# A decoder block's first norm: scale and shift in eight pieces, and a turn of x by diagonal matmuls

## The chip, the cores and the metric

The kernel runs on one core of a Trainium2 chip. A time is the device time of one execution in microseconds; the number compared is the median over several executions. Profiled executions are single ones, with a trace.

## What is computed

A decoder block over 256 tokens of width 1024: a modulated norm, a token mixer (attention and a gated convolution), a second modulated norm and a mixture of 32 experts. The change touches only how the first norm and its modulation are made, ahead of the projection `w_in`:

```
mod = jax.nn.silu(c) @ w_ada[l] + b_ada[l]
sh1, sc1, ga1, sh2, sc2, ga2 = jnp.split(mod, N_MOD, axis=-1)
h = modulate(rms_norm(x, g_norm1[l]), sh1, sc1)    # norm(x) * (1 + sc1) + sh1
z = h @ w_in[l]
```

`c` is one row of 1024, `w_ada` is 1024 x 6144, so `sc1` and `sh1` are 1024 values each, and each needs 1024 x 1024 weights (4 MB).

## The kernel before, in words

**Order of transfers.** All large weights come in through SP's queue, in one list (`stream`), into a ring of slots of 1 MB (`slots`; `pump` at lines 125 to 138 sends as long as a slot is free, `release` frees one and pumps). For the front, `FIRST` (line 40) writes the order by hand: four pieces of 256 columns for the scale (`sc1.i`), four for the shift (`sh1.i`), and eight row blocks of `w_in` for q, k and v (`qkv.k`, 768 KB), mixed as `sc0 sh0 qk0 sc1 qk1 sh1 ...`. Small rows (`c`, `b_ada`, `g_norm1` and others) go through the same queue (`load_rows`, line 222). A DMA of this queue may also have to wait for an earlier DMA's completion, eight places before it in program order: the waits named `DMAHW0` to `DMAHW7`.

**Start.** `x` (two tiles of 128 tokens) is squared on VectorE and ScalarE (lines 353, 355), the inverse root is made (lines 356 to 358), x is scaled by it (`xh`, lines 360, 361) and transposed by 16 TensorE transposes into four PSUM banks (line 365), which VectorE and ScalarE copy to `hf` (lines 372, 374). Between the two halves of the transposes stand the first pieces of scale and shift: `first_ada` (lines 509 to 525) makes eight matmuls of 32 x 256 (four column groups of the array side by side, line 516), copies the bank to `part` and turns it into columns by two matmuls with `sel` (line 501, "cols" below), after which VectorE makes `a1` or `sh1` (lines 504 to 507). `warm(n)` issues n idle matmuls.

**Units.** The front's matmul work is a list of units: 24 for q, k and v (three per k, each six matmuls of 512 columns, line 428, in three products of high and low parts), then 56 for the other projections and more. Each unit's weights are split into a high part by ScalarE (line 396, `sthi`) and a low part by VectorE (line 397, `stlo`), four units ahead at most (`run_units`, lines 401 to 417). Tasks are generators: `after(i, g)` starts one behind unit i, and each unit advances every task by one step, so a task's instructions stand between the units on every engine. `first_scale(i)` and `first_shift(i)` for i = 1 to 3 are such tasks. Scale pieces 2 and 3 are summed on VectorE (`ada_sum`, lines 331, 333), all others on TensorE. `modulate1(k)` (lines 527 to 530) makes the high part of the modulated x on ScalarE, then the value and its low part on VectorE; unit 3k needs them. `small_work` (lines 561 to 576, behind unit 7) transposes small rows in banks 6 and 7.

**Behind the front** come attention, convolution, the second norm, routing (from line 939) and eight rounds of four experts (lines 1049 to 1207), each reading 24 MB of weights through the same ring. `L1027` gathers tokens with matmuls that have a block of x as the stationary operand and 128 columns of a one-hot matrix as the moving one.

```
    for i in range(1, 4):
        after(6 * i - 6, lambda i=i: first_scale(i))
        after(6 * i - 3, lambda i=i: first_shift(i))
```

## Time and profile before

| | |
|---|---|
| median of 3 runs | 663.52 us (663.48 to 663.66) |
| the profiled execution | 665.23 us, of which its span is 663.5 us |
| TensorE busy | 533.8 us (80%) |
| VectorE, ScalarE, GpSimd busy | 195.5, 146.7 and 40.9 us |
| read from HBM | 257.12 MB, 389 GB/s over the span |
| SP's queue | 256.98 MB, 93.4% of 16 engines' span |

The page cuts the span into 40 slices of 16.6 us; a digit is a busy share in tenths. The span begins with the first instruction and ends with the last one; the execution's own time has 1.7 us more around it.

### The profile page before, as it was taken

To read this page: it belongs to the slowest core of one execution; us is meant where nothing else is said; L and a number is where in the kernel's file an instruction comes from. 1 tells how busy PE (TensorE), PEld (TensorE's weight loads), DVE (VectorE), ACT (ScalarE), POOL (GpSimd) and SP (SyncE) were. 2 spreads that over 40 slices of the span, in tenths; PEclk is the share of its full clock that TensorE was granted. 3 is DMA by queue.
4 is the path that set the end of the run, shared out by engine and by line. 5 is a ranking of instruction groups with operands and counts; after the bars stand their busy time and mean duration, and the time that the engine had idled before them with its cause. 6 is when DMAs were issued, how large, how long until landed. Compare 5 with 4: busy or idle time off the path is not lost. (4 is left out here: it accounts for less than half of the span.)

```text
span 663.5 us, 11736 instructions
## 1 busy us (share of the span) xinstructions
PE 533.8 (80%) x5054; PEld 322.1 (49%) x5055; DVE 195.5 (29%) x405; ACT 146.7 (22%) x290; POOL 40.9 (6%) x59
## 2 busy tenths in 40 slices
PE   7999999999999899988575756676766875677765
PEld 6678897988998637363043104301510540161033
DVE  4687449657896412020020001001100100010002
ACT  4536456744555220010010001000000100010001
POOL 0012511500040000000000000000000000000000
PEclk9999999999999898999888799968987596897669
DMA  8999994699959699999999997999999999999996
GB/s 315 426 425 398 426 421 154 244 356 378 399 199 407 282 410 426 425 427 424 428 427 423 423 426 328 423 428 427 425 426 426 428 426 425 428 425 425 427 427 255
DMA packets 37765, 259.01 MB, mean 390 GB/s; under 512 B 4545, under 2 KB 5673, under 8 KB 7242
## 3 DMA queue, kind: packets, MB, share of 16 engines
q1 hardware_dynamic: 36136, 256.98, 93.4%
q10 hardware_dynamic: 1362, 1.05, 0.5%
q8 instruction: 42, 0.69, 0.4%
q0 software_dynamic: 208, 0.15, 0.1%
q14 instruction: 17, 0.14, 0.1%
HBM read 257.12 MB, written 1.05 MB: 389 GB/s over the span
## 5 line engine op out<-in xcount | busy, mean ns | idle before, releaser
L1060 PE MATMUL ps<-slot,xg 128*32 128x512 f32 x1024 | 163.4, 745 | 76.4 <-DMA slot<-in_up_dram 71.4
L1060 PEld LDWEIGHTS ps<-slot,xg 128*32 128x32 f32 x1024 | 26.1, 120 | 197.8 <-DMA slot<-in_up_dram 160.3
L428 PE MATMUL ps<-hbuf,sthi 128*128 128x256 f32 x512 | 94.8, 287 | 0.0
L428 PEld LDWEIGHTS ps<-hbuf,sthi 128*128 128x128 f32 x512 | 79.0, 190 | 11.4 <-ACT sthi L396 6.7
L397 DVE TENSOR_TENSOR stlo<-slot,sthi 128x512 fp32r<-128x512 f32 x100 | 72.0, 723 | 37.9 <-ACT sthi L396 36.7
L396 ACT ACTIVATE sthi<-slot 128x512 fp32r<-128x512 f32 x108 | 68.0, 630 | 62.7 <-PE ps L428 50.2
L1068 DVE TENSOR_TENSOR sl<-sl,ps 128x512 f32<-128x512 f32 x8 | 5.5, 688 | 254.7 <-PE ps L1060 246.4
L1080 PE MATMUL ps<-slot,sl 128*32 128x128 f32 x2048 | 67.9, 287 | 14.6 <-DMA slot<-in_down_dram 9.7
L428 PE MATMUL ps<-hbuf,stlo 128*128 128x256 f32 x256 | 72.2, 282 | 0.7 <-POOL stlo L397 0.7
L1080 PEld LDWEIGHTS ps<-slot,sl 128*32 128x32 f32 x2048 | 57.1, 115 | 29.1 <-DMA slot<-in_down_dram 13.3
L1047 ACT ACTIVATE GW<-ps 128x256 f32<-128x256 f32 x8 | 3.1, 384 | 239.1 <-PE ps L1046 239.1
L1088 PE MATMUL ps<-ysb,GW 128*128 128x512 f32 (+1 forms) x76 | 37.1, 615 | 17.6 <-DVE ysb L1086 17.6
L428 PEld LDWEIGHTS ps<-hbuf,stlo 128*128 128x128 f32 x256 | 48.5, 190 | 0.9 <-POOL stlo L397 0.9
L428 PE MATMUL ps<-sthi,hbuf 128*128 128x512 f32 x128 | 43.2, 404 | 1.1 <-ACT hbuf L528 0.9
L1086 DVE TENSOR_TENSOR ysb<-ps,ga 128x512 f32<-128x512 f32 (+1 forms) x19 | 11.5, 606 | 90.7 <-PE ps L1080 83.7
L1027 PEld LDWEIGHTS ps<-GW,x 128*128 128x128 f32 x256 | 33.4, 212 | 6.4 <-issue 5.6
L1027 PE MATMUL ps<-GW,x 128*128 128x128 f32 x256 | 36.0, 302 | 0.2 <-DVE GW L1018 0.2
L1088 PEld LDWEIGHTS ps<-ysb,GW 128*128 128x128 f32 x76 | 13.3, 203 | 30.9 <-DVE ysb L1086 22.1
L428 PEld LDWEIGHTS ps<-sthi,hbuf 128*128 128x128 f32 x128 | 23.7, 188 | 8.9 <-issue 1.6
L1033 ACT ACTIVATE xg<-ps,sm,sm 128x128 f32<-128x128 f32 x32 | 12.4, 457 | 59.8 <-PE ps L1027 59.8
L428 PE MATMUL ps<-stlo,hbuf 128*128 128x512 f32 x64 | 25.1, 392 | 0.0
L1035 DVE TENSOR_SCALAR xg<-ps,sm,sm 128x128 f32<-128x128 f32 x32 | 11.2, 404 | 35.0 <-PE ps L1027 35.0
(264 smaller groups left out, 429.2 us busy)
## 6 DMA issues: line engine op xcount, KB each, us to landing
slot<-in_up_dram SPq DMA_DIRECT2D x128, 1024.0 KB, 19.6
slot<-in_down_dram SPq DMA_DIRECT2D x64, 1024.0 KB, 19.6
slot<-in_front_dram SPq DMA_DIRECT2D x42, 1024.0 KB, 11.4
slot<-in_front_dram SPq DMA_DIRECT2D x8, 768.0 KB, 14.4
gates<-in_front_dram SPq DMA_DIRECT2D x4, 1024.0 KB, 7.0
x<-in_x_dram SPq DMA_DIRECT2D x2, 512.0 KB, 3.7
out_dram<-x ACTq DMA_DIRECT2D x1, 512.0 KB
out_dram<-x ACTq DMA_DIRECT2D x4, 128.0 KB, 1.8
```

What stands on the lines that cost most here:

```text
L396: S.activation(hi, src, AF.Copy)
L397: (G if i in on_pool else V).tensor_sub(lo, src, hi.bitcast(F32))
L428: PE.matmul(o, l, r, start=start and n == 0, stop=stop and n == 2, skip_group_check=True)
L1027: PE.matmul(o[:, 128 * (k % 4):128 * (k % 4) + 128], x[:, t, 128 * k:128 * k + 128], Gt[:, t, :], start=t == 0, stop=t == 1)
L1033: S.activation(xg[:, k, :], src, AF.Identity, bias=sh2[:, k:k + 1], scale=a2[:, k:k + 1])
L1035: V.tensor_scalar(xg[:, k, :], src, a2[:, k:k + 1], sh2[:, k:k + 1], op0=OP.mult, op1=OP.add)
L1047: S.activation(WT.rearrange("p t n -> p (t n)"), YC[:, :256], AF.Copy)
L1060: PE.matmul(o[js, :], xg[:, k, js], w[:, j, :], start=k == 0, stop=k == DK - 1)
L1068: V.tensor_mul(sl, sl, HB)
L1080: PE.matmul(bank[js, cs], hidT[:, k, js], w[:, 4 * j + k, :], start=k == 0, stop=k == 3, skip_group_check=True)
L1086: V.tensor_mul(ysb[:, cs], (bank or (YC, YD)[n])[:, cs], ga2[:, ns])
L1088: PE.matmul(ACC[t][n][:, cs], WT[:, t, :], ysb[:, cs], start=q == 0, stop=q == NQ - 1, skip_group_check=True)
```

## The change

`FIRST` is gone. The weights for scale and shift are laid out on the host as eight pieces `mod1.i`, each with 128 columns of the scale and 128 of the shift (1 MB), and the transfers alternate `mod1.0 qkv.0 mod1.1 qkv.1 ...`. All eight are summed on TensorE by `first_ada(i)`, one `first_task(i)` per k behind unit 3i - 3, with two cols matmuls, one VectorE instruction for `a1` (with `ab1` made beforehand) and one for `sh1`. `modulate1(i)` follows in the same step. The bank is copied to `part` by VectorE always. x is no longer scaled and transposed: a diagonal matrix of the inverse roots (`dg`, 128 x 128 per tile) is the moving operand of 16 matmuls with x as the stationary one (`x_turn`). The rows `c`, `b_ada`, `g_norm1` are issued by ScalarE, and four large transfers are issued ahead of the other small rows. `warm(4)` is dropped, and a tile of 8 columns that filled space.

```
+    for i in range(DK):
+        f.append((f"mod1.{i}", "mod1", 0, 8, 256 * i, 256))
+        f.append((f"qkv.{i}", "w_in", 128 * i, 1, 0, 1536))
...
-    load_rows("c", SY)
+    load_rows("c", S)
+    load_rows("b_ada", S)
+    load_rows("g_norm1", S)
...
-    load_rows("b_ada", SY)
-    load_rows("g_norm1", SY)
-    pump(1)
+    pump(4)
     for nm in ("g_norm2", "conv_w", "conv_b"):
         load_rows(nm, SY)
-    pump(2)
...
-    xh = [flat(sq), flat(vt)]
-    V.tensor_scalar(xh[0], x[:, 0, :], rinv1[:, 0:1], None, op0=OP.mult)
-    S.activation(xh[1], x[:, 1, :], AF.Copy, scale=rinv1[:, 1:2])
...
+    dg = flat(sq)[:, :256].rearrange("p (t n) -> p t n", t=2)
+    for t in range(2):
+        V.tensor_scalar(dg[:, t], ident, rinv1[:, t:t + 1], None, op0=OP.mult)
+
+    def x_turn(b):
+
+        for k in (2 * b, 2 * b + 1):
+            for t in range(2):
+                PE.matmul(PS[b][:, 256 * (k % 2) + 128 * t:256 * (k % 2) + 128 * t + 128],
+                          x[:, t, 128 * k:128 * k + 128], dg[:, t], start=True, stop=True)
+        d = flat(hf[:, 2 * b:2 * b + 2, :])
+        if b % 2:
+            S.activation(d, PS[b], AF.Copy)
+        else:
+            V.tensor_copy(d, PS[b])
...
+    def first_ada(i):
+
+        bank = B[6 + i % 2]
+        w = cols256(slot(f"mod1.{i}"))
         for kk in range(2):
             for j in range(4):
-                k = 2 * j + kk
+                k = 4 * kk + j
                 PE.matmul(bank[32 * j:32 * j + 32, :256], sil[:, k:k + 1].to_broadcast([128, 32]), w[:, k, :],
                           start=kk == 0, stop=kk == 1)
...
+        release(f"mod1.{i}")
+        p = part[i % 2][:, :256]
+        V.tensor_copy(p, bank[:, :256])
+        yield 1
+        for c in range(2):
+            PE.matmul(bank[:, c:c + 1], p[:, 128 * c:128 * c + 128], sel, start=True, stop=True)
+        V.scalar_tensor_tensor(a1[:, i:i + 1], bank[:, 0:1], col("g_norm1", i, 1), ab1[:, i:i + 1], op0=OP.mult,
+                               op1=OP.add)
+        V.tensor_add(sh1[:, i:i + 1], bank[:, 1:2], col("b_ada", 4 * SH1 + i, 1))
+
+    def first_task(i):
+        yield from first_ada(i)
+        modulate1(i)
...
+    for i in range(1, DK):
+        after(3 * i - 3, lambda i=i: first_task(i))
...
+    first = first_ada(0)
     columns("a", B[4])
+    first_bias()
+    x_turn(0)
+    next(first)
+    for b in range(1, 4):
+        x_turn(b)
+    split_next()
+    next(first, 0)
+    modulate1(0)
+    run_units(20)
...
+    w["mod1"] = np.stack([w["w_ada"][:, 512 * b:512 * b + D].reshape(D, DK, 128) for b in (SC1, SH1)], 2).reshape(D, -1)
```

Where the instructions stand, at three places. **TensorE, from the second half of the transposes to the first unit, before** (`vt` holds the scaled second tile of x; the last row is unit 0):

```order
L501 MATMUL ps_76<-sel,part_219 128x1 x2
L365 MATMUL ps_70<-ident,vt 128x128 x2
L365 MATMUL ps_71<-ident,vt 128x128 x2
L365 MATMUL ps_72<-ident,vt 128x128 x2
L365 MATMUL ps_73<-ident,vt 128x128 x2
L516 MATMUL ps_77<-slot_78,sm_181 32x256 x8
L267 MATMUL ps_75<-ident 128x128 x4
L501 MATMUL ps_77<-sel,part_220 128x1 x2
L428 MATMUL ps_70<-sthi_101,hbuf_99 128x512
```

and the same stretch now, from the first use of x on (`sq` holds the diagonal matrices, `gates_114` is the slot of `mod1.0`):

```order
L359 MATMUL ps_69<-sq,x 128x128 x4
L503 MATMUL ps_75<-gates_114,sm_180 32x256 x8
L359 MATMUL ps_70<-sq,x 128x128 x4
L359 MATMUL ps_71<-sq,x 128x128 x4
L359 MATMUL ps_72<-sq,x 128x128 x4
L510 MATMUL ps_75<-sel,part_218 128x1 x2
L419 MATMUL ps_69<-sthi_100,hbuf_98 128x512
```

The second piece's eight matmuls and the idle matmuls are gone from ahead of unit 0, and the cols follow the last matmul on x.

**VectorE, the same stretch, before** (`sm_221` is `a1`, `sm_222` is `sh1`, `stlo_105` the low part of unit 0's weights):

```order
L374 COPY gates_114<-ps_72 128x512
L521 COPY part_220<-ps_77 128x256
L504 TENSOR_TENSOR sm_222<-ps_77,cols_a 128x2
L397 TENSOR_TENSOR stlo_105<-slot_79,sthi_101 128x512
L529 TENSOR_SCALAR gates_114<-gates_114,sm_221,sm_222 128x256
```

and now (`sm_220` is `a1`, `sm_221` is `sh1`, `sthi_100` the high part of unit 0's weights, `ps_71` the third bank of x):

```order
L507 COPY part_218<-ps_75 128x256
L365 COPY gates_113<-ps_71 128x512
L388 TENSOR_TENSOR stlo_104<-slot_77,sthi_100 128x512
L511 SCALAR_TENSOR_TENSOR sm_220<-ps_75,cols_a,sm_238 128x1
L513 TENSOR_TENSOR sm_221<-ps_75,cols_a 128x1
L521 TENSOR_SCALAR gates_113<-gates_113,sm_220,sm_221 128x256
```

The low part of unit 0's weights stood behind the shift, and stands now ahead of scale and shift.

**TensorE, around `small_work` (behind unit 7), before**, with the waits that each row carries:

```order
L428 MATMUL ps_73<-stlo_108,hbuf_99 128x512
L428 MATMUL ps_73<-sthi_104,hbuf_99 128x512
L256 MATMUL ps_77<-ident,qkb 128x26 [waits DMAHW7_49,DMAHW3_49,DMAHW2_49]
L567 MATMUL ps_76<-qkb,ident 128x128 x2
L428 MATMUL ps_74<-sthi_101,hbuf_99 128x512 [waits Activation_49]
```

and now:

```order
L419 MATMUL ps_72<-sthi_103,hbuf_98 128x512
L510 MATMUL ps_76<-sel,part_219 128x1 [waits DVE_49]
L510 MATMUL ps_76<-sel,part_219 128x1
L248 MATMUL ps_76<-ident,qkb 128x26 [waits DMAHW4_49,DMAHW3_49,DMAHW5_49,DMAHW2_49,DVE_49]
L538 MATMUL ps_75<-qkb,ident 128x128 x2
L419 MATMUL ps_73<-sthi_100,hbuf_98 128x512 [waits Activation_49]
```

The cols of piece 3 now stand right ahead of `small_work` and use its bank, and its first matmul has a wait for VectorE more.

## Rows read from the trace of the kernel before

**Rows 1.** The page, 40 slices of 16.6 us: TensorE busy tenths, and GB/s moved.
```profile
PE   7999999999999899988575756676766875677765
...
GB/s 315 426 425 398 426 421 154 244 356 378 399 199 407 282 410 426 425 427 424 428 427 423 423 426 328 423 428 427 425 426 426 428 426 425 428 425 425 427 427 255
```

**Rows 2.** Waits of SP's queue, 60 to 200 us: us in total, times, longest.
```profile
SPq L137 <- DVE stlo L397: 83.2, 15, 17.6
```

**Rows 3.** Windows: busy us per engine (TensorE first), granted clock, DMA share, GB/s.
```profile
16.72:59.40 42.68, 42.45 (x238) 31.42 (x238) 31.85 (x74) 21.91 (x41) 6.71 (x13) 1.00 1.01 415
100.00:130.00 30.00, 29.02 (x239) 25.05 (x237) 23.39 (x36) 21.02 (x54) 11.48 (x8) 1.00 0.57 214
225.00:227.00 2.00, 2.00 (x13) 1.78 (x16) 0.46 (x2) 0.46 (x1) 0.00 (x0) 0.50 0.03 12
```

**Rows 4.** Timeline, SP's queue, 0 to 120 us: start, us, engine, line, operation, count.
```profile
1.24 0.83 SPq L229 DMA_DIRECT2D x<-in_x_dram  x2
...
9.92 10.17 SPq L137 DMA_DIRECT2D slot<-in_front_dram  x11
```

**Rows 5.** Timeline, 0 to 30 us, the chain up to the first unit.
```profile
6.35 1.06 ACT L355 ACTIVATE gates<-x 128x1024 f32<-128x1024 f32 x1 [1.81 <-DMA x<-in_x_dram]
...
8.56 0.16 DVE L323 SCALAR_TENSOR_TENSOR sm<-sm,sm 128x2 f32<-128x2 f32 x1
...
10.04 1.07 PE L516 MATMUL ps<-gates,sm 128*32 128x256 f32 x16 [1.88 <-ACT vt L361]
...
12.33 1.07 PE L365 MATMUL ps<-ident,vt 128*128 128x128 f32 x8
...
13.00 1.10 ACT L372 ACTIVATE gates<-ps 128x512 f32<-128x512 f32 x2 [1.46 <-PE ps L365]
...
15.49 0.63 ACT L396 ACTIVATE sthi<-slot 128x512 fp32r<-128x512 f32 x1 [1.39 <-DMA slot<-in_front_dram]
...
16.15 0.69 DVE L397 TENSOR_TENSOR stlo<-slot,sthi 128x512 fp32r<-128x512 f32 x1
...
16.72 0.50 PE L428 MATMUL ps<-sthi,hbuf 128*128 128x512 f32 x1 [0.89 <-ACT hbuf L528]
```

**Rows 6.** Timeline of TensorE, 0 to 80 us: a piece, its cols and small_work between units.
```profile
24.62 1.07 PE L516 MATMUL ps<-slot,sm 128*32 128x256 f32 x16
25.62 0.50 PE L428 MATMUL ps<-sthi,hbuf 128*128 128x512 f32 x1
...
27.12 0.50 PE L501 MATMUL ps<-sel,part 128*128 128x1 f32 x4
27.48 0.48 PE L428 MATMUL ps<-sthi,hbuf 128*128 128x512 f32 x1
...
31.91 0.24 PE L256 MATMUL ps<-ident,qkb 26*128 26x26 f32 x1
...
32.61 0.50 PE L428 MATMUL ps<-sthi,hbuf 128*128 128x512 f32 x1
```

**Rows 7.** Timeline, from those cols to the modulated x of k = 2, all engines.
```profile
27.66 0.16 DVE L504 TENSOR_TENSOR sm<-ps,cols_a 128x2 f32<-128x2 f32 x1 [0.27 <-PE ps L501]
...
27.85 0.60 ACT L528 ACTIVATE hbuf<-gates,sm,sm 128x256 fp32r<-128x256 f32 x1 [1.19 <-DVE sm L504]
...
28.94 0.43 DVE L530 TENSOR_TENSOR hbuf<-gates,hbuf 128x256 fp32r<-128x256 f32 x1
...
29.42 0.73 PE L428 MATMUL ps<-sthi,hbuf 128*128 128x512 f32 x2
```

**Rows 8.** Timeline of TensorE, 287 to 292 us: 16 gathering matmuls (two records each), and the next.
```profile
287.58 3.84 PE L1027 MATMUL ps<-GW,x 128*128 128x128 f32 x32
291.35 0.86 PE L1080 MATMUL ps<-slot,sl 128*32 128x128 f32 x24
```

**Rows 9.** Timeline of TensorE, 222 to 231 us, behind the routing.
```profile
222.69 0.18 PE L982 MATMUL ps<-sm,before 128*128 128x32 bf16 x1 [1.64 <-DVE sm L980]
...
224.14 2.77 PE L1027 MATMUL ps<-GW,x 128*128 128x128 f32 x12 [0.24 <-DVE GW L1018]
```

**Rows 10.** Waits of SP's queue, 225 to 245 us.
```profile
SPq L137 <- PE ps L1060: 16.8, 11, 8.6
```

More of the change, by code (lines that the diff above doesn't have):

```diff
@@ L39 @@
 QI, KI, VI, XBI, BGI, CGI, GI = 0, 1, 2, 3, 4, 5, 6
-FIRST = ("sc0 sh0 qk0 sc1 qk1 sh1 qk2 sc2 qk3 sh2 qk4 sc3 qk5 sh3 qk6 qk7").split()
 REST = ("in00 in01 in10 m20 m21 in11 m22 m23 in20 in21 in30 m24 m25 m26 in31 m27 in40 g100 in41 g101 g20 in50 g21 "
@@ L496, in block_kernel, with first_bias @@
             wo_unit(n, k, [B[b] for b in wob[n]])
-    def first_cols(i, shift, bank, p, w):
-        for c in range(2):
-            PE.matmul(bank[:, c:c + 1], p[:, 128 * c:128 * c + 128], w, start=True, stop=True)
-        cs = slice(2 * i, 2 * i + 2)
-        if shift:
-            V.tensor_add(sh1[:, cs], bank[:, :2], col("b_ada", 4 * SH1 + 2 * i, 2))
-        else:
-            V.tensor_add(a1[:, cs], bank[:, :2], col("b_ada", 4 * SC1 + 2 * i, 2))
-            V.scalar_tensor_tensor(a1[:, cs], a1[:, cs], 1.0, col("g_norm1", 2 * i, 2), op0=OP.add, op1=OP.mult)
-    def first_ada(i, shift, bank):
-        key = f"{('sc', 'sh')[shift]}1.{i}"
-        w = cols256(slot(key))
+    ab1 = small([128, 8])
+    def first_bias():
+        V.scalar_tensor_tensor(ab1, col("b_ada", 4 * SC1, 8), 1.0, col("g_norm1", 0, 8), op0=OP.add, op1=OP.mult)
+    def first_ada(i):
+        bank = B[6 + i % 2]
+        w = cols256(slot(f"mod1.{i}"))
         for kk in range(2):
             for j in range(4):
-                k = 2 * j + kk
+                k = 4 * kk + j
                 PE.matmul(bank[32 * j:32 * j + 32, :256], sil[:, k:k + 1].to_broadcast([128, 32]), w[:, k, :],
                           start=kk == 0, stop=kk == 1)
-        release(key)
-        p = part[shift][:, :256]
-        if shift and not i:
-            V.tensor_copy(p, bank[:, :256])
-        else:
-            S.activation(p, bank[:, :256], AF.Copy)
-        yield 1
-        first_cols(i, shift, bank, p, sel)
+        release(f"mod1.{i}")
+        p = part[i % 2][:, :256]
+        V.tensor_copy(p, bank[:, :256])
+        yield 1
+        for c in range(2):
[6 more added lines that the diff above has]
+        modulate1(i)
     def modulate1(k):
@@ L530, in modulate1 @@
         V.tensor_sub(hpart(1, k), hf[:, k, :], hpart(0, k).bitcast(F32))
-    def first_scale(i):
-        if i == 1:
-            yield from first_ada(i, 0, B[6])
-            return
-        p = misc[:, 256 * i:256 * i + 256]
-        w = cols256(slot(f"sc1.{i}"))
-        for k in range(DK):
-            ada_sum(p, w[:, k, :], k, k == 0)
-            if k % 2:
-                yield 1
-        release(f"sc1.{i}")
-        first_cols(i, 0, B[6], p, one)
-    def first_shift(i):
-        yield from first_ada(i, 1, B[7])
-        for k in (2 * i, 2 * i + 1):
-            modulate1(k)
-            yield 1
     ssq = small([128, 2, 2, NH])
@@ L854, in resid_task @@
             yield 1
-    for i in range(1, 4):
-        after(6 * i - 6, lambda i=i: first_scale(i))
-        after(6 * i - 3, lambda i=i: first_shift(i))
+    for i in range(1, DK):
+        after(3 * i - 3, lambda i=i: first_task(i))
     after(24, router_loads)
@@ L887, in more_slots @@
         pump()
-    a, b = first_ada(0, 0, B[6]), first_ada(0, 1, B[7])
+    first = first_ada(0)
     columns("a", B[4])
-    next(a)
-    x_transposes(0)
-    next(a, 0)
-    x_transposes(1)
-    x_copies()
-    next(b)
-    warm(4)
-    next(b, 0)
-    for k in range(2):
-        split_next()
-        modulate1(k)
-    run_units(19)
+    first_bias()
[7 more added lines that the diff above has]
+    run_units(20)
     free.append(RING)
```

18 lines of the change are left out of this document (removed).

## The prediction

> **What bounds the kernel now.** I read the page's slices first. From 240 us on the core moves some 425 GB/s, nearly without a pause, so the end is when the weights have come in; up to then there are holes (154, 244, 199, 282 GB/s) while TensorE is at 9 tenths [rows 1]. The waits of SP's queue say whose holes they are: between 60 and 200 us it waits 83.2 us in 15 pieces for the low-part split of a unit's weights, that is, for a slot to come free [rows 2]. From 100 to 130 us the DMA engines are 0.57 busy and TensorE 29.02 of 30 us; between unit 0 and the end of the q, k and v units TensorE has 42.45 busy of 42.68 us [rows 3]. The last time that compute holds up the transfers is behind the routing, where the queue waits 16.8 us for the first experts' matmuls [rows 10]. So the time is: when TensorE gets through the front, plus a fixed stretch of transfers. TensorE has next to no slack from 16.72 us to there, so a microsecond added to its work in the q, k and v units, or to the start of unit 0, should come out whole at the end. The holes also mean that bytes arriving earlier in the front buy nothing once unit 0 runs.
>
> **When unit 0 starts.** Before: it starts at 16.72 us, released by the modulated x [rows 5].
> Transfers: x is issued at 1.24 us behind `c` [rows 4]; with `c` on ScalarE it goes out at about 0.8, so both tiles should land some 0.45 earlier, the second at 5.9 instead of 6.35. ScalarE issues three DMAs ahead of its table load; silu(c) is then about 1 us later, covered by the 5 us until its first reader. `qkv.0` was issued only at 9.92, since the queue had small rows ahead of it and waited for an earlier transfer [rows 4]; now it is fourth on SP and should land by about 11.5 instead of 15.49.
> From x on: square to inverse root takes 2.37 us (6.35 to 8.72) [rows 5], so 8.3; two diagonals on VectorE (128 columns, 0.2 each, as the 0.16 of a small instruction says), 8.7. Then 16 matmuls with x stationary and 128 moving columns. The gathers have that very shape: 16 of them from 287.58 to 291.35, 0.236 us each [rows 8]. Eight transposes took 1.07 us [rows 5], 0.134 each. Four matmuls to 9.7; piece 0 is there by then (the first piece's matmuls began at 10.04 [rows 5], now issued earlier), 1.0 us to 10.75; twelve more, 2.85 us, to 13.7.
> Here the trace speaks against one page. The Trainium skill, "Perfetto Trace Analysis", section Transposes, asks to use the transpose and not a standard matmul, and "TensorE: Matmul & The Clock Gate", Terms, calls the transpose mode 4x faster for FP32. By that the turn would take 16 x 4 x 0.134 = 8.6 us instead of 3.8, and my sum would be 4.8 higher. I take the row of the gathers, 1.8 times a transpose, since it is of the same shape.
> Now the part that eats the gain: the order on the two engines behind. ScalarE copies the last bank (0.6), then splits unit 0's weights (0.63); VectorE makes their low part (0.69) **ahead of** `a1` and `sh1` (0.16 each), and only then can ScalarE modulate (0.60) [rows 5, 7]. With 0.4 to 0.5 for five hand-overs that is 3.2 us behind 13.7: unit 0 at 16.9 instead of 16.72, **+0.2**. Bounds: if the turn cost no more than transposes, 1.6 less, -1.4 (15.3); if transfers of `mod1.0` and the small rows push x and the piece, +1.2.
>
> **What is added between unit 0 and the end of q, k and v.**
> - Pieces on TensorE: four stood there, seven do now. One is 1.00 us (24.62 to 25.62) [rows 6]: **+3.0**. What they replace, 16 VectorE instructions, lay beside TensorE's work; VectorE was busy 31.85 of 42.68 us and has now less to do [rows 3].
> - Cols: seven groups instead of six, 0.36 each (27.12 to 27.48) [rows 6], and seams of about 0.05 at three more pieces and one more group: **+0.5**.
> - Modulated x: from the cols to its use the chain is 27.66, 27.85, 28.94, and it was ready just in time for the third matmul of its unit at 29.42 [rows 7]. Now VectorE has two instructions there, not one: 0.2 more, plus what was just enough. The cols stand again one unit ahead of the user. So TensorE should wait about 0.25 at each k from 1 to 7 but 3 (where `small_work` stands between): six waits, 1.5, against 0.2 before: **+1.3**. Bounds: 0 (if VectorE reads the cols at once) and 2.6 (twice the wait).
> - `small_work`: its first matmul writes the bank that holds the cols of piece 3, and so waits for VectorE to read both. The first read begins 0.54 behind the start of the cols [rows 7], two reads end near 0.95, TensorE is ready at 0.36: **+0.5**. Behind it, `small_work` itself is as long as before (0.70, 31.91 to 32.61) [rows 6].
> - Splits, the copy of the bank to `part` (VectorE 0.4, was ScalarE's), the later release of slots: nothing; a piece's bank is copied while a unit of 1.4 us runs. If that cover went, it would be some 0.1 per piece.
>
> **The clock.** With piece 1 and the idle matmuls gone, TensorE idles from about 14.1 to 16.9. After 1.64 us of idling at 222.69 the granted clock fell to 0.50 (1.2 of 2.4 GHz) [rows 3, 9]: 12 gathering records took 2.77 us, where 32 take 3.84 at full clock, 1.3 too much [rows 8, 9]. After an idle time of 1.88 us at 10.04 nothing fell: the piece right behind it took 1.07 us, as the one at 24.62 does [rows 5, 6]. So either can happen; the new idle time is longer than both, and part of the loss would hide in unit 0, which waits for its low parts anyway. I take half of 1.3, **+0.6**; bounds -1.3 (no fall here, and the fall at 224 us gone because things shifted) and +1.7.
>
> **Sum:** 0.2 + 3.0 + 0.5 + 1.3 + 0.5 + 0.6 = 6.1 us. The profiled execution took 665.23 us, a span of 663.5 and 1.7 around it, so it would become 671.3. The median of the unprofiled runs, 663.52, is 1.7 lower; the same sum on it gives 663.5 + 6.1 = **669.6 us**, slower by 0.9%. A measurement here tells about 0.2%, 1.3 us, from no change.
>
> **Rivals.**
> 1. *DMA bounds the front (other side).* In the first slice 315 GB/s flowed where 426 can [rows 1]: 1.84 MB, 4.3 us of transfers. The new order closes the hole. If the front ran at the rate of its transfers, the end would come 4.3 earlier, 659.2. It decides if SP's queue is never without work for lack of slots. For it: some 420 GB/s between 17 and 100 us. Against: the 83.2 us of waits for slots. 0.05.
> 2. *The cheap case.* The turn costs what transposes cost, the six waits are absent and the clock stays: -1.4 + 3.0 + 0.5 - 0.2 + 0.5 = 2.4, 665.9. For it: the wait at 29.42 was all but nothing. 0.17.
> 3. *The clock falls and stays low over the first pieces*, with waits at the upper bound: 0.2 + 3.0 + 0.5 + 2.6 + 0.5 + 1.7 = 8.5, 672. 0.10.
> 4. *The turn takes four times a transpose.* 16 x 4 x 0.134 from the row of eight transposes, 4.8 more than in my sum: 674.4. For it: the array may treat a transpose apart. Against: the gathers, at 1.8 times. 0.04. It is what the two pages of the Trainium skill named above would give.
> 5. *It is absorbed.* The fall at 224 us vanishes (-1.3), unit 0 starts at 15.3 and the attention tasks, which follow units and not times, swallow some: within 1.3 us of 663.5. Only two short waits of TensorE would have to give. 0.08.
>
> **How the numbers follow.** My case, 667.4 to 671.6, has 0.56. The range reaches from the cheap case to the top of mine: 665.6 to 671.6, with about 0.8 in it. Faster by more than 0.2%: rival 1 and a corner of 5, 0.06. Within 0.2%: the rest of 5 and a corner of 2, 0.09. Slower: 0.85.
>
> **What would show it.** Right: unit 0 within 0.7 us of 16.9, with VectorE's low part of unit 0 ending just ahead of `a1`; the first unit of the next projection at about 65, not 59.4; seven pieces of 1.0 between; TensorE waiting for VectorE's low part of the modulated x at most k; a wait of half a microsecond at the first matmul of `small_work`; the holes in GB/s up to 230 us still there, all some 6 us later. Wrong: unit 0 near 13, which says that I misread the order on ScalarE and VectorE; a 16-matmul turn of over 8 us; or a q, k and v stretch that is longer by 5 us while the end does not move, which would say that the front has slack that I do not see.

## The result, and the profile after

The changed kernel takes 668.88 us (median of 4 runs, 668.39 to 669.87) where the kernel before takes 663.59 (4 runs, 663.48 to 663.99): a ratio of 1.0080, 95% interval 1.0064 to 1.0096, so it is slower by 5.3 us, 0.8%. The forecast was 669.6. The profiled execution after took 668.64 us, a span of 666.9 and 1.7 around it.

The picture of the whole is the one of before. The page's slices, TensorE busy in tenths and GB/s moved:

```profile
PE   7999999999999898989575667665776785596666
...
GB/s 344 409 425 421 403 373 109 258 287 353 425 246 337 358 379 425 425 427 424 428 427 424 422 428 347 407 427 427 426 426 429 425 425 428 427 426 426 427 427 286
```

The first slice moves 344 GB/s instead of 315 [rows 1], so the transfers do start earlier; the holes up to 230 us are all still there. SP's queue still waits for slots, which VectorE's low-part splits free. Its waits from 60 to 205 us (in total, times, longest), beside [rows 2]:

```profile
SPq L130 <- DVE stlo L388: 81.3, 17, 8.2
```

and from 225 to 250 us, beside [rows 10]:

```profile
SPq L130 <- PE ps L1027: 16.2, 12, 7.4
```

So TensorE still sets the time up to the experts. The windows of the kernel after, in the columns of [rows 3]:

```profile
16.47:65.91 49.44, 48.88 (x289) 33.40 (x290) 28.02 (x69) 21.08 (x37) 7.22 (x13) 0.97 1.01 420
16.50:24.00 7.50, 7.32 (x37) 4.64 (x38) 3.99 (x10) 2.84 (x6) 0.00 (x0) 0.77 0.98 390
222.00:232.00 10.00, 7.81 (x66) 7.02 (x66) 6.49 (x30) 1.93 (x6) 0.00 (x0) 1.00 0.89 371
```

The q, k and v units take 49.44 us instead of 42.68. Two things stand beside that. From 16.5 to 24 us the granted clock is 0.77 on average, where before it was 1.00: it is at its lower level, 0.50, over most of unit 0 and of the first piece. And behind the routing, where before it fell to 0.50 [rows 3], it is now 1.00.

The chain up to unit 0, from the timeline of the kernel after (start, us, engine, line, operation), beside [rows 5]:

```profile
5.86 1.06 ACT L347 ACTIVATE gates<-x 128x1024 f32<-128x1024 f32 x1 [0.61 <-DMA x<-in_x_dram]
...
8.61 1.16 PE L359 MATMUL ps<-sq,x 128*128 128x128 f32 x8
...
9.70 1.07 PE L503 MATMUL ps<-gates,sm 128*32 128x256 f32 x16
...
10.70 2.94 PE L359 MATMUL ps<-sq,x 128*128 128x128 f32 x24
...
13.48 0.51 PE L510 MATMUL ps<-sel,part 128*128 128x1 f32 x4
...
14.24 0.62 ACT L387 ACTIVATE sthi<-slot 128x512 fp32r<-128x512 f32 x1
14.89 0.69 DVE L388 TENSOR_TENSOR stlo<-slot,sthi 128x512 fp32r<-128x512 f32 x1 [1.41 <-ACT sthi L387]
15.50 0.21 DVE L511 SCALAR_TENSOR_TENSOR sm<-ps,cols_a,sm 128x1 f32<-128x1 f32 x1
...
15.81 0.60 ACT L520 ACTIVATE hbuf<-gates,sm,sm 128x256 fp32r<-128x256 f32 x1 [0.95 <-DVE sm L513]
...
16.47 0.50 PE L419 MATMUL ps<-sthi,hbuf 128*128 128x512 f32 x1 [2.48 <-ACT hbuf L520]
```

x lands 0.49 us earlier (5.86, was 6.35). The 16 matmuls that turn x (two records each) take 1.09 us up to 9.70 and 2.78 up to 13.48, 0.24 each. Then TensorE stands still for 2.48 us, while VectorE first makes the low part of unit 0's weights and only then reads the cols. Unit 0 starts at 16.47, 0.25 earlier than before.

Behind it, the first piece, a later one, its cols, and the cols ahead of `small_work` (timeline of TensorE, kernel after), beside [rows 6]:

```profile
19.38 1.60 PE L503 MATMUL ps<-slot,sm 128*32 128x256 f32 x16
20.92 0.50 PE L419 MATMUL ps<-sthi,hbuf 128*128 128x512 f32 x1
...
24.49 0.39 PE L419 MATMUL ps<-stlo,hbuf 128*128 128x512 f32 x1
24.84 0.73 PE L419 MATMUL ps<-sthi,hbuf 128*128 128x512 f32 x2
...
25.64 0.39 PE L419 MATMUL ps<-sthi,hbuf 128*128 128x512 f32 x1
25.96 1.07 PE L503 MATMUL ps<-slot,sm 128*32 128x256 f32 x16
26.96 0.50 PE L419 MATMUL ps<-sthi,hbuf 128*128 128x512 f32 x1
27.30 0.39 PE L419 MATMUL ps<-stlo,hbuf 128*128 128x512 f32 x1
27.53 0.63 PE L419 MATMUL ps<-sthi,hbuf 128*128 128x512 f32 x2
...
34.51 0.50 PE L510 MATMUL ps<-sel,part 128*128 128x1 f32 x4
35.38 0.24 PE L248 MATMUL ps<-ident,qkb 26*128 26x26 f32 x1 [0.38 <-DVE sm L513]
```

and the first piece behind unit 0 in the trace of before:

```profile
18.81 1.07 PE L516 MATMUL ps<-slot,sm 128*32 128x256 f32 x16
```

Unit 0 takes 2.91 us up to the first piece (16.47 to 19.38) where before it took 2.09 (16.72 [rows 5] to 18.81), and that piece 1.54 instead of 1.00: the low clock costs 0.82 + 0.54 = 1.36. At full clock a piece is 1.00 again (25.96 to 26.96). Around it there are seams: two matmuls of a unit start 0.23 apart (27.30 to 27.53), but the piece starts 0.32 behind the last of them, and the second matmul behind the piece 0.34 behind the first. That is 0.09 + 0.11 = 0.20 per piece. `small_work` starts 0.87 behind the cols, where a matmul that has nothing to wait for starts 0.36 behind them [rows 6], because it waits for VectorE.

Last, behind the routing (timeline of TensorE, kernel after), beside [rows 9]:

```profile
229.20 0.18 PE L949 MATMUL ps<-sm,before 128*128 128x32 bf16 x1 [1.64 <-DVE sm L947]
...
230.66 1.93 PE L994 MATMUL ps<-GW,x 128*128 128x128 f32 x12 [0.24 <-DVE GW L985]
...
235.01 1.92 PE L1027 MATMUL ps<-slot,xg 128*32 128x512 f32 x16
```

The same idle time of 1.64 us is followed by 12 gathering records in 1.93 us instead of 2.77. The last line is the experts' second round; the first and the second in the trace of before:

```profile
226.84 2.36 PE L1060 MATMUL ps<-slot,xg 128*32 128x512 f32 x16
...
229.78 1.92 PE L1060 MATMUL ps<-slot,xg 128*32 128x512 f32 x16
```

All kernels of this study side by side, each from its one profiled execution, the median of all its runs, and the ratio on record, worked out from all runs of the kernel and of the kernel before on the same chip (whose median was 663.1 to 664.0 there). It is not the quotient of the two medians, and differs from it by up to 0.1%. "Idle" is TensorE's idle time just ahead of unit 0; "clock" is the mean granted clock from 16.5 to 24 us; "qkv end" is the first matmul of the next projection; "experts" is the first expert's first matmul; "routing" says whether the gathers in front of it took about 1.9 (full clock) or 2.6 to 3.0 us (low).

| kernel | idle | clock | unit 0 | qkv end | experts | routing | median | ratio, 95% interval |
|---|---|---|---|---|---|---|---|---|
| before | 0.89 | 1.00 | 16.72 | 59.40 | 226.84 | low | 663.59 | |
| after | 2.48 | 0.77 | 16.47 | 65.91 | 232.51 | full | 668.88 | 1.0080 (1.0064 to 1.0096) |
| E1 cols ahead of the split | 1.42 | 0.77 | 15.47 | 65.16 | 231.78 | full | 667.96 | 1.0053 (1.0034 to 1.0073) |
| E2 idle time filled | 0.1 | 1.00 | 16.54 | 64.64 | 231.23 | full | 667.69 | 1.0070 (1.0046 to 1.0093) |
| E3 pieces twice | 2.48 | 1.00 | 16.63 | 70.67 | 237.27 | full | 674.91 | 1.0173 (1.0149 to 1.0198) |
| E4 two pieces on VectorE | 2.48 | 0.77 | 17.04 | 68.82 | 236.46 | low | 672.92 | 1.0134 (1.0109 to 1.0158) |
| E5 unit 0 early | 0 | 1.00 | 14.24 | 61.78 | 228.40 | full | 665.18 | 1.0023 (1.0012 to 1.0035) |
| E6 queue alone | 0.89 | 1.00 | 16.88 | 59.56 | 227.19 | low | 662.65 | 0.9983 (0.9969 to 0.9997) |
| E7 turn alone | 0.89 | 1.00 | 18.73 | 61.38 | 228.99 | low | 664.19 | 1.0011 (1.0001 to 1.0021) |
| E8 mix | 0 | 1.00 | 14.42 | 60.61 | 227.23 | full | 663.79 | 0.9999 (0.9987 to 1.0011) |
| E9 order and queue | 0.50 | 1.00 | 14.52 | 57.73 | 224.31 | full | 661.95 | 0.9974 (0.9963 to 0.9986) |
| E10 order alone | 0.99 | 0.77 | 16.23 | 60.50 | 227.75 | low | 664.29 | 1.0001 (0.9986 to 1.0016) |
| E11 pieces sooner | 0 | 1.00 | 15.25 | 61.15 | 227.75 | full | 663.78 | 0.9999 (0.9987 to 1.0010) |
| E12 fewer filling products | 0.50 | 1.00 | 16.25 | 58.92 | 225.53 | full | 661.70 | 0.9977 (0.9963 to 0.9991) |

From "qkv end" to "experts" it is 166.6 us in every trace with a full clock at the routing and 167.3 to 167.6 in every one with a low clock there, whatever was changed in front. So whatever the q, k and v units lose or gain reaches the experts whole.

### The profile page after: what moved, and what is told of

It is laid out like the page before. It is cut to its first block, busy times and chain, and to the rows that moved or that the text cites. A ratio compares the mean times of both kernels' runs of the same rounds, so it can differ in the third digit from the quotient of the medians.

```text
span 666.9 us, 11810 instructions
## 1 busy us (share of the span) xinstructions
PE 535.1 (80%) x5094; PEld 324.9 (49%) x5095; DVE 191.9 (29%) x402; ACT 144.4 (22%) x284; POOL 41.4 (6%) x59
## 3 DMA queue, kind: packets, MB, share of 16 engines
q10 hardware_dynamic: 1458, 1.09, 0.5%
## 5 line engine op out<-in xcount | busy, mean ns | idle before, releaser
L1027 PE MATMUL ps<-slot,xg 128*32 128x512 f32 x1024 | 158.8, 724 | 81.0 <-DMA slot<-in_up_dram 75.9
L388 DVE TENSOR_TENSOR stlo<-slot,sthi 128x512 fp32r<-128x512 f32 x97 | 68.5, 715 | 37.6 <-ACT sthi L387 36.9
L387 ACT ACTIVATE sthi<-slot 128x512 fp32r<-128x512 f32 x105 | 66.0, 630 | 59.3 <-PE ps L419 49.2
L419 PE MATMUL ps<-sthi,hbuf 128*128 128x512 f32 x128 | 45.6, 416 | 2.7 <-ACT hbuf L520 2.5
```

Of the source, the lines that this page charges most:

```text
L387: S.activation(hi, src, AF.Copy)
L388: (G if i in on_pool else V).tensor_sub(lo, src, hi.bitcast(F32))
L419: PE.matmul(o, l, r, start=start and n == 0, stop=stop and n == 2, skip_group_check=True)
L1027: PE.matmul(o[js, :], xg[:, k, js], w[:, j, :], start=k == 0, stop=k == DK - 1)
```

## The experiments

**E1, the order behind the turn.** Edit of the kernel after: the cols of piece 0, `a1` and `sh1` come ahead of the split of unit 0's weights.

```
-    split_next()
     next(first, 0)
+    split_next()
```

> The changed kernel with one line moved: the cols of piece 0, a1 and sh1 stand ahead of the split of unit 0's weights, so that VectorE makes a1 and sh1 before the low part. Theory (order on ScalarE and VectorE sets the start of unit 0, and the front passes everything on): a1 is made from 14.0 us on, ScalarE modulates right behind its split, which ends at 14.86; unit 0 starts at about 15.6 instead of 16.47. The end moves by the same 0.9, to 668.0; if the shorter idle time (1.6 instead of 2.5 us) leaves the clock up, by 1.3 more, to 666.7. Rival (the front is bound by its transfers): 668.9, no change, wherever unit 0 starts.

Measured, timeline of TensorE in E1:

```profile
13.55 0.50 PE L510 MATMUL ps<-sel,part 128*128 128x1 f32 x4
15.47 0.51 PE L419 MATMUL ps<-sthi,hbuf 128*128 128x512 f32 x1 [1.42 <-ACT hbuf L520]
```

Unit 0 starts 1.00 earlier at the same turn, and q, k and v end 0.75 earlier, the experts start 0.73 earlier. So the low part of the weights did stand in the chain with a whole microsecond, and most of what is gained there is passed on. The clock was low here too, behind an idle time of 1.42.

**E2, the clock at unit 0.** Edit of the kernel after: ten idle products behind the cols, which nothing reads.

```
     next(first, 0)
+    warm(10)
     modulate1(0)
```

> The changed kernel with ten idle matmuls (0.24 us each by the turn's rows) behind the cols of piece 0, where TensorE idles for 2.5 us ahead of unit 0. Theory: the start of unit 0 stays at 16.5 (within 0.2), the granted clock stays at 1.00 through unit 0 and piece 1, and these two take 2.1 and 1.0 us instead of 2.9 and 1.5; the end moves by 1.3, to 667.6, unless the clock falls behind the routing, as it did in the kernel before and not in the changed one, which would give those 1.3 back. Rival (the low clock hides in waits that unit 0 has anyway): 668.9.

Measured, window of E2 in the columns of [rows 3]:

```profile
16.50:24.00 7.50, 7.28 (x42) 4.83 (x43) 5.33 (x13) 3.94 (x7) 0.00 (x0) 1.00 0.97 383
```

Unit 0 starts at the same time (16.54), but the clock is 1.00 and q, k and v end 1.27 earlier, close to the 1.36 counted from the rows of after; so the rival fell, and next to nothing of the low clock hides in waits. The experts start 1.28 earlier. Its median against that of after is inside the two intervals: 1.3 us is about what such a comparison can tell here, and the trace is the better witness.

**E3, each piece twice.** Edit of the kernel after: pieces 1 to 7 repeat their eight matmuls into the unused half of their bank.

```
+        for kk in range(2 if i else 0):
+            for j in range(4):
+                k = 4 * kk + j
+                PE.matmul(bank[32 * j:32 * j + 32, 256:512], ...)
```

> The changed kernel with the eight matmuls of pieces 1 to 7 made twice (the second time into unused columns of the bank): 7 x 1.0 us more on TensorE between unit 0 and the end of q, k and v, nothing else. Theory (a microsecond of TensorE there is a microsecond at the end): the stretch takes 56.4 instead of 49.4 us, and the time is 668.9 + 7.0 = 675.9, plus or minus 1.3 for the clock behind the routing. Rival (the front is bound by its transfers, or has slack behind): 668.9 to 671.

Measured, timeline of TensorE in E3 (its clock from 16.5 to 24 us is in the table):

```profile
16.63 0.50 PE L419 MATMUL ps<-sthi,hbuf 128*128 128x512 f32 x1 [2.48 <-ACT hbuf L525]
...
18.66 1.07 PE L503 MATMUL ps<-slot,sm 128*32 128x256 f32 x16
19.55 1.05 PE L508 MATMUL ps<-slot,sm 128*32 128x256 f32 x16
20.53 0.50 PE L419 MATMUL ps<-sthi,hbuf 128*128 128x512 f32 x1
```

A doubled piece takes 1.87 (18.66 to 20.53), 0.87 more, seven of them 6.1. Q, k and v end 4.76 later than in after: 6.1 less the 1.36 of the clock, which did not fall in this execution. The experts start 4.76 later, and the median is 6.0 us above that of after. The traced execution (673.66) is 1.25 below E3's median, which would fit a fall of the clock in most of the others; no trace shows it. There is no slack for TensorE in this stretch: a microsecond is a microsecond. That also ends rival 1: if transfers bounded the front, doubled pieces would have hidden. And the clock did not fall behind the very idle time, 2.48 us, behind which it fell in after.

**E4, two pieces on VectorE.** Edit of the kernel after: pieces 3 and 6 are summed by VectorE (eight multiply-adds of 256 columns), begun six units ahead of their use, with the cols right behind the last sum.

```
-        yield from first_ada(i)
+        yield from (first_sum(i) if i in ON_DVE else first_ada(i))
...
-        after(3 * i - 3, lambda i=i: first_task(i))
+        after(3 * i - (6 if i in ON_DVE else 3), lambda i=i: first_task(i))
```

> The changed kernel with pieces 3 and 6 summed on VectorE, as two pieces of the scale were in the kernel before (eight sums of 256 columns each, about 0.49 us, spread over four units, and a cols with a column of ones). Theory: TensorE loses two pieces of 1.0 us and their seams (0.2 each): the stretch from unit 0 takes 47.0 instead of 49.4 us and the time is 668.9 - 2.4 = 666.5. Rival (VectorE, which then has 3.9 us more in two of the steps of 6 us, becomes the bound): no gain or a loss, with TensorE waiting for the low parts of weights.

Measured, waits of TensorE in E4, 15 to 72 us (in total, times, longest):

```profile
PE ps L518 <- DVE misc L326: 2.8, 2, 1.4
```

and a window of E4 in the columns of [rows 3]:

```profile
56.00:59.50 3.50, 3.50 (x10) 2.71 (x9) 2.15 (x5) 1.75 (x3) 0.00 (x0) 0.51 1.00 421
```

The rival held in that there was a loss and TensorE waited for VectorE, though for its sums and not for the low parts of weights. Two pieces fewer on TensorE should give 2.4 with their seams, and the sums come 1.4 us late, twice: VectorE does them between the splits of the weights, and the cols stood right behind the last one. Behind the second of these waits (1.36) the clock fell once more, to 0.51 from 56 to 59.5 us, and the 12 matmuls up to the next piece took 4.5 us (from 55.55), where the same 12 take 3.2 behind another piece (from 43.03); behind the first (1.39) it did not fall. Unit 0 was 0.57 later in this execution, and q, k and v ended 2.9 us later than in after: these terms give 2.3 of the 2.9, and the rest is not accounted for. What TensorE is relieved of must also be early on the engine that takes it.

**E5, unit 0 early.** Edit of the kernel after: the cols of piece 0 come ahead of the matmuls on columns 512 and on of x, the matmuls on columns 256 and on go into banks that unit 0 does not use, and three of the four copies stand behind the first modulate.

```
+    x_turn(0, PS[0], V)
     next(first)
+    x_turn(1, PS[4])
+    next(first, 0)
+    x_turn(2, PS[5])
+    x_turn(3, PS[3])
     split_next()
     modulate1(0)
+    x_copy(1, PS[4], V)
+    x_copy(2, PS[5], S)
+    x_copy(3, PS[3], S)
```

> The change, with unit 0's sums begun before the whole of x has been turned: the matmuls that turn columns 256 and on of x are issued behind piece 0 and the matmuls with one column, into banks that unit 0 does not use, and three of the four copies come behind the first modulate. Theory (the path from x to the first unit runs through TensorE's 24 remaining matmuls, the columns, the split and the modulate, and the clock falls because TensorE then stands still for 2.5 us): unit 0 starts at about 13.9 instead of 16.47, the matmuls of x fill the idle time so that the clock stays at 1.00 in 16.5:24, and q, k and v end at about 65.9 - 2.5 - 1.3 = 62.1; whole kernel about 665.0, with 1.3 either way for the clock behind the routing. Rival (the chain of weight transfers or the weights' splits release the units): unit 0 starts early, but waits of the same size follow in units 1 to 4, and q, k and v end at 65 to 66.

Measured: unit 0 at 14.24, no idle time ahead of it, clock 1.00, q, k and v end at 61.78 (expected 62.1), 665.18 us (expected 665.0). The theory of the start holds: the path ran through the turn, the split and the idle time, and the idle time cost the clock as well. Compared with the kernel before, unit 0 is now 2.5 us earlier and q, k and v still end 2.4 later: the stretch behind unit 0 is 47.54 us where it was 42.68, at full clock. Those 4.9 us are the pieces and their company, less some 0.5 that unit 0 no longer waits for its low parts (1.57 up to the first piece, 2.09 before).

**E6, the queue's part alone.** Edit of the kernel before: the three rows on ScalarE's queue, four large transfers right behind x.

```
-    load_rows("c", SY)
+    load_rows("c", S)
+    load_rows("b_ada", S)
+    load_rows("g_norm1", S)
...
-    load_rows("b_ada", SY)
-    load_rows("g_norm1", SY)
-    pump(1)
+    pump(4)
...
-    pump(2)
```

> The kernel before, with the queue's part of the change alone: the rows c, b_ada and g_norm1 on ScalarE's queue, and the first weight transfers issued right behind x. Theory (TensorE bounds the front, transfers do not): x lands some 0.45 us earlier, unit 0 starts at about 16.3 instead of 16.72, and the end moves by the same 0.4, to about 663.2. Rival 1 of the prediction (transfers bound the front): q, k and v end 4 us earlier, 659 in all.

Measured, timeline of TensorE in E6:

```profile
3.52 6.54 PE L266 MATMUL ps<-ident 128*128 128x128 f32 x32
```

In this execution unit 0 was not earlier (16.88): the 32 records of filling products at the start took 6.54 us, where they took 5.45 in the traced execution of before, and the turned row and piece 0 stood behind them. The 12 runs are 0.17% faster all the same by the ratio, 1.1 us, which is more than the 0.4 expected, and the traced execution (663.62) is 1.0 above their median. That the other executions start sooner is likely but not shown. Rival 1 would have given 4 us; it did not come.

**E7, the turn alone.** Edit of the kernel before: the diagonal matrices and 16 matmuls in place of the scaled x and 16 transposes (the expectation says 32 of each; 32 is the number of the matmuls' records).

```
-    xh = [flat(sq), flat(vt)]
-    V.tensor_scalar(xh[0], x[:, 0, :], rinv1[:, 0:1], None, op0=OP.mult)
-    S.activation(xh[1], x[:, 1, :], AF.Copy, scale=rinv1[:, 1:2])
+    dg = flat(sq)[:, :256].rearrange("p (t n) -> p t n", t=2)
+    for t in range(2):
+        V.tensor_scalar(dg[:, t], ident, rinv1[:, t:t + 1], None, op0=OP.mult)
...
-            PE.transpose(PS[k // 2][...], xh[t][:, 128 * k:128 * k + 128], ident)
+            PE.matmul(PS[k // 2][...], x[:, t, 128 * k:128 * k + 128], dg[:, t], start=True, stop=True)
```

> The kernel before, with the turn of x alone changed: 32 matmuls with the diagonal matrices in place of the two scaled copies of x and 32 transposes. Theory (a turn by a matmul takes 0.24 us where a transpose takes 0.13, and 16 or so of them stand in the chain to unit 0; the two diagonal matrices take 0.5 us less than the scaled copies): the chain is some 1.7 us longer at most, unit 0 starts at 17.0 to 18.4, end at 663.9 to 665.3. Rival (a matmul costs four times a transpose): 0.54 each, unit 0 starts some 6.5 us later, end near 670.

Measured, timeline of TensorE in E7:

```profile
10.13 1.07 PE L516 MATMUL ps<-gates,sm 128*32 128x256 f32 x16 [1.16 <-DMA gates<-in_front_dram]
11.13 2.05 PE L365 MATMUL ps<-sq,x 128*128 128x128 f32 x16
13.02 0.51 PE L501 MATMUL ps<-sel,part 128*128 128x1 f32 x4
```

and the instruction behind the second eight transposes of [rows 5] (12.33) in the trace of before:

```profile
13.33 1.07 PE L516 MATMUL ps<-slot,sm 128*32 128x256 f32 x16
```

Eight products (16 records) take 1.9 us up to the next instruction, 0.24 each, where eight transposes took 1.0. Unit 0 starts 2.0 us later (18.73, above the expected 17.0 to 18.4), since the earlier diagonal matrices buy nothing: piece 0 waits for its transfer. The trace's q, k and v end 1.98 later; the ratio is 0.1%, 0.7 us, and the medians differ by 0.2 only, so the executions without a trace lose less than this one. Four times a transpose is excluded.

**E8, an attempt at a faster version.** Edit of E5: pieces 4 and 7 on VectorE, begun seven units ahead with two units between the last sum and the cols, `small_work` behind unit 8, the copy of the bank on ScalarE.

```
-        after(3 * i - 3, lambda i=i: first_task(i))
+        after(3 * i - (7 if i in ON_DVE else 3), lambda i=i: first_task(i))
...
-    after(7, small_work)
+    after(8, small_work)
```

> The early start of the kernel above, and three more edits: pieces 4 and 7 are summed on VectorE, begun four units sooner, with two units between the last sum and the matmuls with one column; small_work stands behind unit 8 instead of unit 7; the copy of a piece's sums out of the bank is ScalarE's for pieces 1 to 7. Theory (each piece on TensorE costs its 1.00 us and its seams, and the trial with pieces 3 and 6 on VectorE failed because TensorE waited for the last sum): two pieces fewer give 2 x 1.2, small_work 0.5, so about 665.0 - 2.9 = 662.1, below the kernel before. Rival (VectorE's sums delay the splits of the weights wherever they stand, and TensorE waits for the splits): TensorE waits on VectorE's low parts by 2 us and more between 24 and 66, and the time stays at or above that of the kernel above.

Measured, waits of TensorE in E8, 12 to 72 us:

```profile
PE ps L424 <- DVE hbuf L549: 0.7, 2, 0.6
```

Between the two. TensorE no longer waits for a sum, and `small_work`'s wait is gone, but the low part of a modulated x is late by 0.6 us, at the place where VectorE does the rows of `small_work` as well. Q, k and v end 1.17 earlier than in E5, not 2.9, and the waits that the view names are only part of what is missing; the time is that of before (0.9999).

**E9, another order of the work before, with the queue's part.** Edit of E6: the transposes of the first tile, both pieces of 256 columns one behind the other, and the transposes of the second tile ahead of, between and behind the cols, where TensorE idled or ran filling products.

```
-    next(a)
     x_transposes(0)
-    next(a, 0)
-    x_transposes(1)
-    x_copies()
+    next(a)
     next(b)
-    warm(4)
+    x_transposes(1, range(2))
+    x_copy(0, V)
+    next(a, 0)
+    x_transposes(1, range(2, 5))
     next(b, 0)
-    for k in range(2):
-        split_next()
-        modulate1(k)
+    x_transposes(1, range(5, 8))
+    split_next()
+    modulate1(0)
+    x_copy(1, V)
+    x_copy(2, S)
+    split_next()
+    modulate1(1)
+    x_copy(3, S)
```

> The kernel before, with the queue's part of the change and another order of the same work in front of unit 0: the transposes of the first half of the tokens, then both sums over 256 columns one behind the other, and the transposes of the other half between and behind the matmuls with one column, where before TensorE waited (0.89 and 0.23 us) or ran four filling products. Theory (what holds unit 0 is TensorE's work in front of it plus the time in which it stands still, and that time can be filled): unit 0 at about 14.5 instead of 16.72, no wait behind it, q, k and v end at about 57.3, the whole kernel about 2 us under the kernel before, 661.7. Rival 1 (the slot with the shift's columns lands too late for its sum to follow at once): TensorE waits for a transfer between 11 and 13 and unit 0 stays at 16 or later. Rival 2 (the early units meet weights that are not split yet): waits on sthi or stlo in units 1 to 4, and q, k and v end above 58.5.

Measured, timeline of TensorE in E9:

```profile
14.52 0.50 PE L429 MATMUL ps<-sthi,hbuf 128*128 128x512 f32 x1 [0.50 <-ACT hbuf L529]
```

Unit 0 at 14.52, q, k and v end at 57.73 (expected 57.3; TensorE waits 0.35 once, at 19.57, for the copy of a piece's sums), 661.95 us: 0.26% below the kernel before, and the fastest whole kernel here.

**E10, the order without the queue's part.** Edit of the kernel before: the order of E9.

> The same order of the work in front of unit 0 with the queues as in the kernel before. Theory: the order alone gives the 2 us, and the queue's part, which the kernel with it alone did not turn into an earlier unit 0 (16.88), adds no more than 0.5: unit 0 at 14.5 to 15.0, about 661.7 to 662.2. Rival (without the earlier issue the slot with the shift's columns lands late): TensorE waits for that transfer, unit 0 at 16 or later, 663 to 664.

Measured, timeline of TensorE in E10:

```profile
12.34 1.07 PE L518 MATMUL ps<-slot,sm 128*32 128x256 f32 x16 [0.62 <-DMA slot<-in_front_dram]
...
16.23 0.50 PE L430 MATMUL ps<-sthi,hbuf 128*128 128x512 f32 x1 [0.99 <-ACT hbuf L530]
```

The rival held: without the earlier issue the second piece waits for its transfer, unit 0 gains 0.5 only, the clock falls behind it (0.77 in the table), and no gain is left (ratio 1.0001). Order and queue give the gain together.

**E11, the price of the wait at each k.** Edit of E5: pieces 2 to 7 begin one unit sooner.

```
-        after(3 * i - 3, lambda i=i: first_task(i))
+        after(3 * i - 4 if i > 1 else 0, lambda i=i: first_task(i))
```

> The changed kernel with the early start, and each piece from 2 on begun one unit sooner, so that a whole unit lies between its matmuls with one column and the first unit that takes the x it modulates. Theory (a piece costs its sums, the seams, and some 0.12 us of waiting for the low part of the modulated x; small_work waits 0.4 for the bank of the piece just ahead of it): the six waits of 0.12 and small_work's 0.4 go, q, k and v end at about 61.78 - 1.1 = 60.7, about 664.1. Rival (the excess of the units beside the pieces is the seams' own, the interruption of the row of 512-column matmuls): only small_work's 0.4 goes, q, k and v end at 61.4, 664.8. If the pieces' slots land late: TensorE waits for a transfer.

Measured: the starts of pieces 5 and 6 in the timeline of E5, and then in that of E11:

```profile
40.95 1.07 PE L507 MATMUL ps<-slot,sm 128*32 128x256 f32 x16
...
47.00 1.07 PE L507 MATMUL ps<-slot,sm 128*32 128x256 f32 x16
```
```profile
39.52 1.07 PE L507 MATMUL ps<-slot,sm 128*32 128x256 f32 x16
...
45.35 1.07 PE L507 MATMUL ps<-slot,sm 128*32 128x256 f32 x16
```

Three units and a piece take 6.05 us in E5 and 5.83 in E11, so the modulated x cost 0.2 at each k: a wait of 0.12, and about as much again in the matmul behind it, as behind any gap. The stretch of q, k and v is 45.90 instead of 47.54: six times 0.2, and `small_work`'s 0.4. The filling products happened to end 1.0 later in E11's traced execution (unit 0 at 15.25), so only 0.63 of the 1.64 shows in the row of q, k and v's end. The time is that of before (0.9999).

**E12, fewer filling products.** Edit of E9: 12 in place of 16 at the start, and the turn of the rows `b_ada` and `g_norm1` behind the first transposes. In this kernel the turned rows are written over part of a bank that holds columns of x, so that these columns are other numbers.

```
-    warm(16)
+    warm(12)
...
-    columns("a", B[4])
     x_transposes(0)
+    columns("a", B[4])
```

> The kernel with the other order of work in front of unit 0 and the queue's part of the change, with 12 filling products in place of 16 ahead of the first row that TensorE turns, and the turn of the rows b_ada and g_norm1 moved behind the first transposes of x. Theory (the filling products end between 7.7 and 10.0 in the traces taken, since TensorE takes up to twice as long for each until it reaches its full rate, and in some executions they end after the scaled x is ready at 9.2, and hold all that follows): the first transposes start at 9.2 to 9.3 whatever that rate, unit 0 at 14.3 to 14.5, q, k and v end at 57.5 to 57.7; the median some 0.3 us under 661.95 and the runs closer together. Rival (fewer filling products leave TensorE longer below its full rate): the transposes of x and the first sums take 1.5 times as long or more, unit 0 at 15 or later, 662.5 or more.

Measured, timeline of TensorE and one window of E12:

```profile
2.48 4.51 PE L266 MATMUL ps<-ident 128*128 128x128 f32 x24
9.24 1.97 PE L366 MATMUL ps<-ident,sq 128*128 128x128 f32 x8 [2.25 <-DVE sq L359]
```
```profile
10.00:11.00 1.00, 1.00 (x6) 0.81 (x4) 0.00 (x0) 0.00 (x0) 0.00 (x0) 0.50 1.03 430
```

In the traced execution the rival's loss came in another way: TensorE idled 2.25 us ahead of the transposes, the granted clock fell to 0.50, the transposes took 1.9 instead of 1.0, and unit 0 started at 16.25. That execution took 663.22 us; the median is 661.70, not to be told from E9's. Half of the runs are below 661.3 and half above 662.1, which would fit a loss in some executions and not in others; only the one has a trace. Nothing is won in the middle.

## Why the prediction was right

It was right in sign and, with 0.7 us, in size. Step by step, with what the traces give up to the end of q, k and v:

| term | forecast | measured |
|---|---|---|
| start of unit 0 | +0.2 | -0.25 |
| three pieces more on TensorE | +3.0 | +3.0 |
| cols and seams | +0.5 | +0.9 |
| wait for the modulated x | +1.3 | +1.0 |
| `small_work`'s wait | +0.5 | +0.5 |
| clock at unit 0 | | +1.36 |
| clock behind the routing | | -1.28 |
| both clock terms | +0.6 | +0.1 |

The first six rows give 6.5, the end of q, k and v moved by 65.91 - 59.40 = 6.51, and the experts' second round (the first is itself slow before) from 229.78 to 235.01, by 5.23; the difference of -1.28 is put down to the clock behind the routing. (The value for cols and seams is the rest of the 6.51; counted from the rows it is 3 x 0.20 + 0.36 + 0.10 = 1.06.) The medians differ by 5.3, so the transfers behind pass the loss on all but unchanged, as the prediction said. The two traced spans differ by 3.4 only: of the 5.23, 4.70 reach the last matmuls (from 658.34 before, from 663.04 after), and from there to the end the traced execution of before, which was itself 1.7 above its median, takes 5.2 us, where after and E6 take 3.9.

- **Start of unit 0.** The chain was as told: transfers 0.49 earlier, 0.24 per product, VectorE's low part ahead of `a1`. The hand-overs behind the turn took 0.2 less than I allowed (13.48 to 16.47 is 2.99, not 3.2) and the turn itself ended 0.2 earlier. E1 shows that the order alone costs 1.0.
- **The turn.** The row of the gathers was the right price. The 0.134 of a transpose was read from the length of a merged row (1.07); from start to start eight take 1.00, 0.125 each, so a product costs 1.9 times a transpose (E7), where the prediction said 1.8. The Trainium skill, "TensorE: Matmul & The Clock Gate", section Terms, calls the transpose mode 4x faster for FP32; the 1.9 measured here decides. The Trainium skill, "Perfetto Trace Analysis", section Transposes, asks to use the transpose for a transposition and gives no factor, so the price of rival 4 rests on the section Terms alone; E7 agrees with the advice in direction, with unit 0 later by 2.0. Whether the transposes of the kernel before run in that mode, no trace here shows.
- **Pieces.** Right: 1.00 each at full clock, and E3 shows that they pass on whole.
- **Cols and seams.** Too small by 0.4. I put a seam at 0.05; a piece between two units costs 0.20, and cols 0.10, on top of their own time. The trace of before had it: its piece at 24.62 [rows 6] also starts 0.32, and not 0.23, behind the matmul ahead of it:

```profile
24.30 0.39 PE L428 MATMUL ps<-sthi,hbuf 128*128 128x512 f32 x1
```

- **Modulated x.** I said 0.25 at each of six k; E11 shows 0.2. The gap before its use (0.35 from 24.49 to 24.84, where 0.23 is usual) is 0.12 of it; the rest is in the matmuls behind the gap, of which two take 0.73 (24.84), where 0.63 is usual (27.53).
- **Clock.** The weakest step: I took half of one fall. In the trace both things happened that my bounds were made of, a fall at unit 0 (+1.36, E2 confirms 1.3) and none behind the routing (-1.28). They nearly cancel. That was luck: with one of the two alone the term would have been off by 0.8 or by 1.9. The price of a fall, 1.3, was right partly by chance: I took it from the gathers alone by counting records, but they were 0.84 slower (2.77 against 1.93), and the rest was in the experts' first round (2.36 against 1.92). What the clock did in the executions without a trace is not shown.
- **The sum.** The errors of the terms (-0.45, +0.4, -0.3 and -0.5) add up to the 0.9 between 6.1 and 5.23 and cancel in part.
- **Rivals.** 1 fell with E3 and E6. 2 needed no waits and no fall at unit 0; both came. Of 3 the fall came, but ended within the first piece, and the waits stayed far from its upper bound. 4 fell with E7. Of 5 only the vanished fall came.

## What to carry to other kernels

Where one engine is busy without a gap and everything behind it only waits for its end, price an edit by what that engine gains or loses, seams included: here 0.2 us for a piece and 0.1 for its cols between large matmuls, beside their own time. Look at the engine's idle time in front of that stretch before the stretch itself: filling it with work that has to be done anyway moved its start by 2.2 us (E5, and E9 with the earlier transfers), and the clock stayed up. And an order pays only if its inputs come in time: neither E10's order nor E6's queue moved unit 0 by more than 0.5 us, together they moved it by 2.2.

## What the runs showed that I had not expected

- **The same idle time, two clocks.** TensorE's granted clock fell behind 2.48 us of idling in after and E4 and not in E3; within E4 it fell behind a wait of 1.36 and not behind one of 1.39. It fell behind 1.42 in E1 and 0.99 in E10 (where 0.62 of waiting stood a few us ahead of that), and never where unit 0 had 0.89 or less ahead of it. Behind the routing the idle time is 1.63 to 1.65 in every trace and the gathers take 1.9 us in nine kernels and 2.6 to 3.0 in five, on both sides of the change. What decides between them is open; the idle time alone does not. So a fall of the clock is a term with two values, not a price.
- **The filling products are not of fixed length.** 32 records took from 5.26 us (E3) to 6.59 (E4, E8) at the start of the kernel. In every trace they start 0.21 us apart at first and 0.11 later, and the step comes between 5.5 us (E3) and 9.2 (E6). The windows give a granted clock of 1.00 ahead of the step, but that is no measurement: each trace's first record of the clock stands at the step, at full clock, and a time without records is counted as 1.00. The factor of 1.9 is about that between the two levels, so the kernel seems to start at the lower one. Where the filling products end, between 7.7 and 10.1 us, can hold piece 0, and explains why the traced unit 0 of E6 and E11 came up to a microsecond later than expected.
- **VectorE's help is dear.** Two pieces moved to it saved TensorE 2 us and more of matmuls. In E4 all of that and more was lost again, by two waits for VectorE and a fall of the clock behind one of them; in E8 more than half, of which 0.7 are waits for VectorE that the trace names.
